# Low parts of split float32 weights: a subtraction on VectorE, or a negated copy on ScalarE and an adding DMA

## Chip, cores and metric

The kernel runs on one core of one Trainium2 chip. The metric is the device time of one execution in microseconds (us); the median of the runs counts.

## What is computed

One decoder layer for 512 tokens of width 1024, all in float32:

```python
h = x + 0.5 * swiglu(rmsnorm(h, ffn1_norm), w_gate, w_up, w_down)        # d_ff 2816
aq, ak, av, gq, gk, gv, glr, gog = split_cols(rmsnorm(h, mix_norm) @ w_in)
attn_o = sliding_window_attention(rope(aq), rope(ak), av, sinks)          # 8 heads of 64, window 128
gla_o  = rmsnorm(gla_chunked(gq, gk, gv, log_alpha), gla_out_norm) * silu(gog)
h = h + concat([attn_o, gla_o]) @ w_out
h = h + 0.5 * swiglu(rmsnorm(h, ffn2_norm), ...)                          # second feed-forward
h = h + sigmoid(rmsnorm(h, ple_gate_norm) @ ple_w_gate) * rmsnorm(p @ ple_w_proj, ple_norm)
```

## The kernel before

Every matmul of weights with activations is made of three on TensorE. Weight and activation are each held as a pair (`hi`, `lo`) of type float32r whose sum is the float32 value, and `mm3` adds hi x hi, hi x lo and lo x hi into one PSUM tile. So each weight must be loaded, cast to `hi`, and its rest computed as `lo`, before TensorE can use all of it.

The class `Weights` does that for all 88 units of up to 1 MB, in the order of their use. `load` starts a unit's DMA from DRAM on SP's queue into a raw tile `wraw`; there are two raw buffers, so the load of a unit waits until the unit two before it has been split. `split` makes one or two ring tiles of 128x1024 out of a unit (170 in all): ScalarE casts into `whi` (line 87), then VectorE writes `wlo` = raw - hi (line 88; GpSimd for units 2 and 3). Ring tiles lie in two rings, `whi` and `wlo`, of 5 buffers each. A new tile can only be written when TensorE has finished with the tile that had its buffer. `get` asks for splits up to 4 units ahead.

A unit is cut in one of two ways. `add_cols` units (gate and up weights, `in` columns of the mixer) hold 8 row blocks by 256 columns; a ring tile is 128 of these columns, so in the raw tile it is 8 separate pieces of 128 floats per partition. `add_rows` units (down projection, the other mixer weights, `w_out`, the last gate) give ring tiles of two whole row blocks of 512 columns, contiguous in the raw tile.

A feed-forward (`ffn`) runs over three groups of 8, 8 and 6 blocks of 128 hidden columns (`GROUPS`). For each pair of blocks TensorE goes through four ring tiles one after the other (gate, up, gate, up; PSUM tiles `pg`, `pu`), each with 24 matmuls of 512 columns. ScalarE and VectorE turn the results into the activation pairs `ahi`, `alo`. Then the down projection of the group: for each half of the output columns (c0 = 0, 512) four ring tiles (three in the last group) are used together by four GEMMs, one for each 128 tokens (PSUM tile `pd`). A GEMM takes the tiles in turn, six matmuls each, so the buffers of the four tiles come free one after the other while the fourth GEMM runs. The mixer and `w_out` use sets of four tiles in the same way (`gemm_ts`).

The order of instructions on each engine is set when the program is built, by a scheduler that places instructions by a timeline of its own; each engine then works through its list in order and waits on semaphores. GpSimd's list holds the powers of the row norms (`rs_...`, line 203) and some DMAs; SP's the loads.

Of the kernel before, what the change touches and what calls it, by code (L numbers as in the profile page):

```python
# [8 lines left out]
F32 = mybir.dt.float32  # L9
# [3 lines left out]
ALU = mybir.AluOpType  # L13
AX = mybir.AxisListType

P = 128
# [12 lines left out]
class Weights:  # L29
    """Streams weight units from DRAM and splits each into two float32r parts whose sum is the float32 weight."""  # L30

# [11 lines left out]
    def add_cols(self, name, w, c0, nf):  # L43
        """[1024, nf*128] columns: one ring tile [P, 8, 128] per 128 columns."""
        keys = [(name, c0 // P + i) for i in range(nf)]
        src = w[:, c0:c0 + nf * P].rearrange("(k p) c -> p k c", p=P)
        self.add(keys, [P, KC, nf * P], [(slice(0, P), src)], [
            (lambda r, i=i: r[:, :, i * P:(i + 1) * P]) for i in range(nf)])

    def add_rows(self, name, w, k0, nk, c0, n, tag=None):  # L50
        """nk row blocks of 128 by n columns: one ring tile [P, 2, n] per two row blocks."""
        src = w[k0 * P:(k0 + nk) * P, c0:c0 + n].rearrange("(k p) c -> p k c", p=P)
        keys = [(name, c0 if tag is None else tag, k0 + i) for i in range(0, nk, 2)]
        self.add(keys, [P, nk, n], [(slice(0, P), src)], [
            (lambda r, i=i: r[:, i:i + 2, :]) for i in range(0, nk, 2)])
# [16 lines left out]
    def split(self):  # L72
        nc = self.nc
        u = self.done
        while self.loaded <= u:
            self.load()
        keys, shape, loads, views = self.units[u]
        raw = self.raws[u]
        self.done += 1
        for i, (k, view) in enumerate(zip(keys, views)):  # L80
            v = view(raw)
            a, b = v.shape[1], v.shape[2]
            hi_t = self.ringp.tile([P, 1024], F32R, name=f"whi{u}_{i}", tag="whi")
            lo_t = self.ringp.tile([P, 1024], F32R, name=f"wlo{u}_{i}", tag="wlo")
            hi = hi_t[:, :a * b].rearrange("p (a b) -> p a b", a=a)
            lo = lo_t[:, :a * b].rearrange("p (a b) -> p a b", a=a)
            nc.scalar.copy(hi, v)  # L87
            (nc.gpsimd if u in (2, 3) else nc.vector).tensor_tensor(lo, v, hi.bitcast(F32), op=ALU.subtract)  # L88
            self.tiles[k] = (hi, lo)
# [8 lines left out]
def hymba_kernel(tc, A, out):  # L98
    nc = tc.nc
# [29 lines left out]
    def mm3(o, l, r, start, stop_):  # L129
        """o += l.T @ r where l and r are (hi, lo) pairs."""  # L130
        mm(o, l[0], r[0], start, False)
        mm(o, l[0], r[1], False, False)
        mm(o, l[1], r[0], False, stop_)

# [1 line left out]
    idn = cst.tile([P, P], F32, name="idn")  # L136
# [13 lines left out]

# [1 line left out]
    def add_ffn(i):  # L152
# [38 lines left out]

# [1 line left out]
    last_pow = [None]  # L193
# [6 lines left out]
    def rms_scale(ms, n, name):  # L200
        """(mean square + eps) ** -0.5"""
        rs = small(f"rs_{name}", n)
        last_pow[0] = nc.gpsimd.tensor_tensor(rs, ms, nhalf[:, :n], op=ALU.pow).ins
        return rs

    def norm(t, gain, nT, name):
        """Row norm of h[t], to be transposed into columns t*128.. of the (hi, lo) pair nT."""
        nrm = w4(f"nrm_{name}{t}")
        ss = small(f"ss_{name}{t}", 2)
        for c in range(2):  # L210
            sl = slice(c * 512, c * 512 + 512)
            nc.scalar.activation(nrm[:, sl], h[t][:, sl], AF.Square, scale=1.0 / 32.0, accum_out=ss[:, c:c + 1])
        ms = small(f"ms_{name}{t}", 1)
        nc.vector.scalar_tensor_tensor(ms, ss[:, 0:1], EPS, ss[:, 1:2], ALU.add, ALU.add)
        rs = rms_scale(ms, 1, f"{name}{t}")
        nc.vector.scalar_tensor_tensor(nrm, h[t], rs, gain, ALU.mult, ALU.mult)
        return t, nrm, nT, name
# [18 lines left out]
    def gemm_ts(ps, xT, t, tiles):  # L236
        """ps[tokens of t, n] = x[t] @ W, with x's transpose stationary; tiles hold two row blocks each."""
        n = len(tiles)
        for j, (wh, wl) in enumerate(tiles):
            for i in range(2):  # L240
                k = 2 * j + i
                mm3(ps, (xT[0][:, k, tokens(t)], xT[1][:, k, tokens(t)]), (wh[:, i, :], wl[:, i, :]),
                    k == 0, k == 2 * n - 1)
# [45 lines left out]

# [1 line left out]
    emb_d = [drp.tile([P, D], F32, name=f"emb_d{t}") for t in range(NT)]  # L291
# [45 lines left out]

# [1 line left out]
    consts = tc.issue_after(W.last_dma)  # L339
# [34 lines left out]

# [1 line left out]
    with tc.tile_pool(name="ffn1p", bufs=1, reuse_waits="tile") as fp:  # L376
# [13 lines left out]

# [1 line left out]
    hpool.close()  # L392
# [12 lines left out]
    def head_scale(src, name):  # L405
        """Per row and head of 64: (sum of squares + 64 eps) ** -0.5"""
        sq = t2(f"sq_{name}")
        nc.scalar.activation(sq, src, AF.Square)
        ss = small(f"qs_{name}", 8)
        nc.vector.reduce_sum(ss, heads(sq), AX.X)  # L410
        nc.vector.tensor_scalar_add(ss, ss, 64.0 * EPS)
        return rms_scale(ss, 8, f"q_{name}")

    def rotate(x, tab, wide, name):
        """Rotary embedding of x (views by wide) with the gains folded into the tables."""
        t1 = t2(f"r1_{name}")
# [7 lines left out]

    # keys, values and gate ranks of all tokens
    kall = t2("kall")
# [19 lines left out]

    # log decays of the recurrence and their running sums within chunks of 128 tokens
    glT = t2("glT")[0:17, :]
# [25 lines left out]

    # sliding-window attention; query heads are kept as pairs (h, h + 4), one per key head
    qTs = {}
# [71 lines left out]

    # gated linear attention
    gqT = mp.tile([P, 2, S], F32, name="gqT")  # L550
# [30 lines left out]

    # decayed scores of each chunk, transposed, by halving: pairs split at the middle of blocks of 2s tokens
    Ac = [mp.tile([P, 8, 64], F32, name=f"Ac{p}") for p in range(2)]
# [49 lines left out]

    # decayed queries, keys and the state after each chunk
    qb = mp.tile([P, 2, S], F32, name="qb")
# [132 lines left out]

# [1 line left out]
    hp = hpool.enter_context(tc.tile_pool(name="hp2", bufs=1, reuse_waits="tile"))  # L770
# [28 lines left out]

# [1 line left out]
    with tc.tile_pool(name="outp", bufs=1, reuse_waits="tile") as op:  # L801
# [30 lines left out]
def _constants():  # L832
    """Tables that depend on the shapes alone: rotary angles and masks."""
    f = np.float32
# [45 lines left out]
```

## Time and profile before

| | us |
|---|---|
| median of 3 runs (lowest, highest) | 1035.73 (1035.29, 1036.16) |
| profiled execution, first to last instruction | 1034.1 |
| TensorE busy | 1020.0 |
| VectorE busy | 457.8 |
| ScalarE busy | 352.9 |
| GpSimd busy | 45.9 |
| line 87, cast to `whi`, 170 on ScalarE | 176.5 |
| line 88, `wlo`, 166 on VectorE | 200.5 |

For the profiled execution the trace gives its span from first to last instruction; the median of the runs is 1.6 us more, which lies around the span. The busy times are sums over the span and overlap each other. Matmuls are pipelined: one is listed with 0.39 us although the next begins 0.23 us after it, so rates are read from distances between starts.

### The profile page before, as it was taken

What the parts mean: (1) busy time and instruction counts of PE and PEld (TensorE: products, weight loads), DVE (VectorE), ACT (ScalarE), POOL (GpSimd) and SP (SyncE); (2) the same over time, 40 slices, a digit from 0 to 9 for tenths busy, and PEclk for the clock granted to TensorE, in tenths of its full rate; (3) what the DMA queues carried; (4) which work ended last, traced back from release to release, by engine and by line L of the source; (5) the groups of instructions that cost most, each with busy time, mean ns of one, the idle gap of its engine ahead of it and who ended that gap; (6) DMA issues with size and microseconds to landing.
All of it is one profiled execution on the core that took longest, in us unless ns stands there. A gap on an engine that the chain in (4) does not pass through costs nothing.

```text
span 1034.1 us, 12380 instructions
## 1 busy us (share of the span) xinstructions
PE 1020.0 (99%) x5210; PEld 840.9 (81%) x5210; DVE 457.8 (44%) x610; ACT 352.9 (34%) x559; POOL 45.9 (4%) x58
## 2 busy tenths in 40 slices
PE   7999999999999999999999999999999999999998
PEld 5988888888888889887667779888888888888887
DVE  5533224333343346577876464332343323432553
ACT  6533113321132225554465243221132311332441
POOL 3300000000000001100000110000000000000100
PEclk9999999999999999999999999999999999999999
DMA  6842223322233234130203323332242222423231
GB/s 243 273 137 82 82 82 126 118 82 82 82 123 102 82 114 153 42 123 4 79 22 82 123 89 110 107 96 68 82 158 86 84 79 82 138 86 102 90 145 52
DMA packets 78203, 105.78 MB, mean 102 GB/s; under 512 B 5682, under 2 KB 55107, under 8 KB 78147
## 3 DMA queue, kind: packets, MB, share of 16 engines
q1 hardware_dynamic: 75842, 96.60, 28.6%
q0 software_dynamic: 2304, 8.39, 2.2%
q8 instruction: 41, 0.67, 0.3%
q14 instruction: 16, 0.12, 0.0%
HBM read 98.69 MB, written 6.29 MB: 102 GB/s over the span
## 4 chain that ended last, share of the span: by engine, by line
PE 97%; DVE 1%; ACT 1%; DMA 0%; issue 0%; SPq 0%
PE pg L127 23%; PE pu L127 23%; PE pd L127 23%; PE pgt L127 4%; PE wo L127 4%; PE gog L127 2%; PE gv L127 2%; PE gqk L127 2%; PE aq L127 2%; PE gr L127 1%; PE sc L127 1%; PE pv L127 1%; PE kvr L127 1%; PE o L127 1%; PE pe L127 1%; PE pt L540 1%
## 5 line engine op out<-in xcount | busy, mean ns | idle before, releaser
L87 ACT CAST whi<-wraw 128x1024 fp32r<-128x1024 f32 (+1 forms) x170 | 176.5, 1043 | 505.8 <-PE pg L127 144.7
L88 DVE TENSOR_TENSOR wlo<-wraw,whi 128x1024 fp32r<-128x1024 f32 (+1 forms) x166 | 200.5, 1212 | 215.1 <-ACT whi L87 205.4
L127 PE MATMUL pg<-nhi_f,whi 128*128 128x512 f32 (+1 forms) x384 | 143.3, 373 | 2.3 <-ACT nhi_f L196 2.3
L127 PE MATMUL pg<-nlo_f,whi 128*128 128x512 f32 (+1 forms) x384 | 143.6, 374 | 0.0
L127 PE MATMUL pu<-nhi_f,whi 128*128 128x512 f32 (+1 forms) x384 | 142.8, 372 | 0.5 <-DVE h L784 0.5
L127 PE MATMUL pg<-nhi_f,wlo 128*128 128x512 f32 (+1 forms) x384 | 143.1, 373 | 0.0
L127 PE MATMUL pu<-nlo_f,whi 128*128 128x512 f32 (+1 forms) x384 | 142.8, 372 | 0.0
L127 PE MATMUL pu<-nhi_f,wlo 128*128 128x512 f32 (+1 forms) x384 | 142.6, 371 | 0.0
L127 PE MATMUL pd<-whi,ahi 128*128 128x512 f32 x352 | 137.3, 390 | 0.2
L127 PE MATMUL pd<-wlo,ahi 128*128 128x512 f32 x352 | 137.0, 389 | 0.0
L127 PE MATMUL pd<-whi,alo 128*128 128x512 f32 x352 | 136.0, 389 | 0.0
L269 DVE TENSOR_TENSOR af<-pu,sg 128x512 f32<-128x512 f32 x44 | 30.4, 691 | 137.1 <-PE pu L127 136.7
L127 PEld LDWEIGHTS pg<-nhi_f,whi 128*128 128x128 f32 x384 | 72.7, 189 | 15.3 <-ACT nhi_f L196 3.0
L127 PEld LDWEIGHTS pu<-nhi_f,whi 128*128 128x128 f32 x384 | 72.5, 189 | 13.1 <-DVE h L784 0.7
L127 PEld LDWEIGHTS pg<-nhi_f,wlo 128*128 128x128 f32 x384 | 72.9, 190 | 12.6
L127 PEld LDWEIGHTS pg<-nlo_f,whi 128*128 128x128 f32 x384 | 72.8, 190 | 12.6 <-DVE nlo_f L197 0.2
L127 PEld LDWEIGHTS pu<-nlo_f,whi 128*128 128x128 f32 x384 | 72.5, 189 | 12.5
L127 PEld LDWEIGHTS pu<-nhi_f,wlo 128*128 128x128 f32 x384 | 72.3, 188 | 12.5
L286 DVE SCALAR_TENSOR_TENSOR h<-pd,h 128x512 f32<-128x512 f32 x48 | 33.1, 689 | 108.8 <-PE pd L127 108.8
L127 PEld LDWEIGHTS pd<-whi,ahi 128*128 128x128 f32 x352 | 66.1, 188 | 14.6 <-DVE h L286 1.1
L127 PEld LDWEIGHTS pd<-whi,alo 128*128 128x128 f32 x352 | 66.1, 188 | 13.8
L127 PEld LDWEIGHTS pd<-wlo,ahi 128*128 128x128 f32 x352 | 66.1, 188 | 13.6
(228 smaller groups left out, 1167.6 us busy)
## 6 DMA issues: line engine op xcount, KB each, us to landing
wraw<-in_ffn_w_gate_dram SPq DMA_DIRECT2D x22, 1024.0 KB, 5.1
wraw<-in_ffn_w_up_dram SPq DMA_DIRECT2D x22, 1024.0 KB, 5.2
wraw<-in_ffn_w_down_dram SPq DMA_DIRECT2D x20, 1024.0 KB, 5.0
wraw<-in_w_in_dram SPq DMA_DIRECT2D x8, 1024.0 KB, 5.2
wraw<-in_ple_w_gate_dram SPq DMA_DIRECT2D x4, 1024.0 KB, 5.3
h<-in_x_dram SPq DMA_DIRECT2D x4, 512.0 KB, 8.5
emb_d<-eo POOLq DMA_DIRECT2D x4, 512.0 KB, 4.6
wraw<-in_ffn_w_down_dram SPq DMA_DIRECT2D x4, 512.0 KB, 3.5
```

Of the source, the lines that this page charges most:

```text
L87: nc.scalar.copy(hi, v)
L88: (nc.gpsimd if u in (2, 3) else nc.vector).tensor_tensor(lo, v, hi.bitcast(F32), op=ALU.subtract)
L127: nc.tensor.matmul(o, lhsT=l, rhs=r, start=start, stop=stop_, **kw)
L269: nc.vector.tensor_mul(af, pu, sg)
L286: nc.vector.scalar_tensor_tensor(hs, ps, 0.5, hs, ALU.mult, ALU.add)
L540: nc.tensor.transpose(pt[:, tokens(a)], e[:, a, kb * P:(kb + 1) * P], idn)
```

## The change

Only `Weights.split` changes (and comments go, which moves later lines by 6). Units 0 and 1 and the last four (the whole last gate) keep the subtraction on VectorE, units 2 and 3 the one on GpSimd. For the other 80 units ScalarE writes the negated raw weights, rounded to float32r, into `wlo`; then a DMA on GpSimd's queue adds the raw weights to them in place, from SBUF to SBUF. So `wlo` again holds the weight less its rounding.

```diff
@@ Weights.split
             nc.scalar.copy(hi, v)
-            (nc.gpsimd if u in (2, 3) else nc.vector).tensor_tensor(lo, v, hi.bitcast(F32), op=ALU.subtract)
+            if u in (0, 1) or u > len(self.units) - 5:
+                nc.vector.tensor_tensor(lo, v, hi.bitcast(F32), op=ALU.subtract)
+            elif u in (2, 3):
+                nc.gpsimd.tensor_tensor(lo, v, hi.bitcast(F32), op=ALU.subtract)
+            else:
+                nc.scalar.mul(lo, v, -1.0)
+                nc.gpsimd.dma_start(out=lo.bitcast(F32), in_=v, accum_op=ALU.add)
```

The program then has 156 such copies on ScalarE (line 93) and 156 such DMAs on GpSimd (line 94): 88 of 128x8x128, 64 of 128x1024, 4 of 128x544. VectorE has 10 subtractions left. In the changed program SP's loads wait on the semaphores of these DMAs, where they waited on VectorE before.

ScalarE, first feed-forward, between the halves of the first group's down projection. The names are ring tiles (`whi`, `wlo`) and raw tiles (`wraw`) with their buffer numbers. Before:

```order
L272 CAST ahi_7_1049<-af_7_1047 128x512
L87 CAST whi_1_923<-wraw_917 128x1024
L87 CAST whi_0_929<-wraw_927 128x1024
L87 CAST whi_1_933<-wraw_927 128x1024
L87 CAST whi_0_1055<-wraw_1053 128x1024
```

In the changed program:

```order
L278 CAST ahi_7_1069<-af_7_1067 128x512
L93 ACTIVATE wlo_1_941<-wraw_933 128x1024
L87 CAST whi_1_940<-wraw_933 128x1024
L93 ACTIVATE wlo_0_948<-wraw_945 128x1024
L87 CAST whi_0_947<-wraw_945 128x1024
L93 ACTIVATE wlo_1_953<-wraw_945 128x1024
L87 CAST whi_1_952<-wraw_945 128x1024
L87 CAST whi_0_1075<-wraw_1073 128x1024
```

Each tile now has two instructions here, and the one for the low part stands ahead of the cast.

TensorE, at the start of the second half of the same down projection (`pd_0_512_0` is the GEMM of the first 128 tokens, `pd_0_512_1` of the next). Before, from the second tile's last matmuls on:

```order
L127 MATMUL pd_0_512_0_1197<-wlo_1_924,ahi_3_777 128x512
L127 MATMUL pd_0_512_0_1197<-whi_1_923,alo_3_778 128x512
L127 MATMUL pd_0_512_0_1197<-whi_0_929,ahi_4_905 128x512
L127 MATMUL pd_0_512_0_1197<-wlo_0_930,ahi_4_905 128x512
L127 MATMUL pd_0_512_0_1197<-whi_0_929,alo_4_906 128x512
L127 MATMUL pd_0_512_0_1197<-whi_0_929,ahi_5_913 128x512
L127 MATMUL pd_0_512_0_1197<-wlo_0_930,ahi_5_913 128x512
L127 MATMUL pd_0_512_0_1197<-whi_0_929,alo_5_914 128x512
```

In the changed program:

```order
L133 MATMUL pd_0_512_0_1225<-wlo_1_941,ahi_3_789 128x512
L133 MATMUL pd_0_512_0_1225<-whi_1_940,alo_3_790 128x512
L133 MATMUL pd_0_512_0_1225<-whi_0_947,ahi_4_921 128x512
L133 MATMUL pd_0_512_1_1251<-whi_0_935,ahi_0_641 128x512
L133 MATMUL pd_0_512_1_1251<-wlo_0_936,ahi_0_641 128x512
L133 MATMUL pd_0_512_1_1251<-whi_0_935,alo_0_642 128x512
...
L133 MATMUL pd_0_512_1_1251<-whi_1_940,alo_3_790 128x512
L133 MATMUL pd_0_512_1_1251<-whi_0_947,ahi_4_921 128x512
L133 MATMUL pd_0_512_0_1225<-wlo_0_948,ahi_4_921 128x512
```

After one matmul with the third tile's high part the next GEMM's first 12 matmuls, on the two tiles that are there, now go ahead of the third tile's low part.

TensorE, at the start of the second group's gate and up. Before, behind the 24 matmuls of the first gate tile:

```order
L127 MATMUL pg_8_1321<-nhi_f_96,wlo_0_1056 128x512
L127 MATMUL pu_8_1322<-nhi_f_96,whi_0_1065 128x512
L127 MATMUL pu_8_1322<-nlo_f_97,whi_0_1065 128x512
L127 MATMUL pu_8_1322<-nhi_f_96,wlo_0_1066 128x512
L127 MATMUL pu_8_1322<-nhi_f_96,whi_0_1065 128x512
L127 MATMUL pu_8_1322<-nlo_f_97,whi_0_1065 128x512
```

In the changed program:

```order
L133 MATMUL pg_8_1353<-nlo_f_97,whi_0_1075 128x512
L133 MATMUL pg_8_1353<-nhi_f_96,wlo_0_1076 128x512
L133 MATMUL pu_8_1354<-nhi_f_96,whi_0_1087 128x512
L133 MATMUL pu_8_1354<-nlo_f_97,whi_0_1087 128x512
L133 MATMUL pg_9_1355<-nhi_f_96,whi_1_1080 128x512
L133 MATMUL pg_9_1355<-nlo_f_97,whi_1_1080 128x512
...
L133 MATMUL pg_9_1355<-nlo_f_97,whi_1_1080 128x512
L133 MATMUL pg_9_1355<-nhi_f_96,wlo_1_1081 128x512
L133 MATMUL pg_9_1355<-nhi_f_96,whi_1_1080 128x512
```

Seven matmuls of the second gate tile (`pg_9`) have moved between the first two of the up tile (`pu_8`) and the first that needs its low part.

GpSimd, at the start of the second feed-forward: the reads of h, then the powers of its row norms (`rs_f`). Before:

```order
L773 DMA h_2_4427<-h_d_401 128x1024
L773 DMA h_3_4428<-h_d_402 128x1024
L203 TENSOR_TENSOR rs_f_4616<-ms_f_4614,nhalf 128x1
L203 TENSOR_TENSOR rs_f_4651<-ms_f_4649,nhalf 128x1
L203 TENSOR_TENSOR rs_f_4700<-ms_f_4698,nhalf 128x1
L143 DMA gain_ple_gate_norm<-in_ple_gate_norm_dram 128x1024
L203 TENSOR_TENSOR rs_f_4749<-ms_f_4747,nhalf 128x1
```

In the changed program:

```order
L94 DMA wlo_0_4533<-wraw_4530 128x8x128
L94 DMA wlo_1_4538<-wraw_4530 128x8x128
L209 TENSOR_TENSOR rs_f_4714<-ms_f_4712,nhalf 128x1
L209 TENSOR_TENSOR rs_f_4749<-ms_f_4747,nhalf 128x1
L209 TENSOR_TENSOR rs_f_4798<-ms_f_4796,nhalf 128x1
L94 DMA wlo_0_4545<-wraw_4542 128x8x128
L94 DMA wlo_1_4550<-wraw_4542 128x8x128
L94 DMA wlo_0_4661<-wraw_4658 128x8x128
L149 DMA gain_ple_gate_norm<-in_ple_gate_norm_dram 128x1024
L209 TENSOR_TENSOR rs_f_4847<-ms_f_4845,nhalf 128x1
```

Adding DMAs of 128x8x128 now stand ahead of the powers and, three of them, between the third and the fourth.

## Rows read from the trace of the kernel before

**Rows 1.** Page: busy us, share, instructions per engine; then the chain by engine.

```profile
PE 1020.0 (99%) x5210; PEld 840.9 (81%) x5210; DVE 457.8 (44%) x610; ACT 352.9 (34%) x559; POOL 45.9 (4%) x58
...
PE 97%; DVE 1%; ACT 1%; DMA 0%; issue 0%; SPq 0%
```

**Rows 2.** Windows by stage: stretch, us, busy us by engine, clock, DMA.

```profile
core 0: us, PE busy (x) PEld busy (x) DVE busy (x) ACT busy (x) POOL busy (x), PEclk, DMA share, GB/s
0.00:20.00 20.00, 14.58 (x56) 11.85 (x57) 11.27 (x16) 10.74 (x24) 2.40 (x10) 1.00 0.87 315
20.00:45.00 25.00, 22.83 (x170) 21.99 (x169) 11.66 (x17) 15.86 (x32) 14.89 (x11) 0.93 0.60 194
45.00:380.00 335.00, 334.90 (x1504) 278.19 (x1504) 120.00 (x137) 91.06 (x113) 1.20 (x3) 1.00 0.32 103
...
560.00:640.00 80.00, 78.17 (x441) 66.33 (x441) 41.66 (x65) 27.89 (x52) 9.35 (x13) 1.00 0.31 103
640.00:990.00 350.00, 349.89 (x1570) 290.21 (x1569) 131.15 (x146) 99.34 (x129) 4.32 (x8) 1.00 0.32 105
990.00:1034.00 44.00, 39.63 (x203) 33.48 (x201) 17.17 (x25) 9.67 (x15) 0.00 (x0) 1.00 0.13 51
```

**Rows 3.** Timeline of PE: start us, us, line, operation, out<-in, shapes.

```profile
111.64 0.39 PE L127 MATMUL pu<-nhi_f,whi 128*128 128x512 f32 x1
...
117.08 0.39 PE L127 MATMUL pd<-whi,ahi 128*128 128x512 f32 x1
...
138.84 0.39 PE L127 MATMUL pd<-whi,ahi 128*128 128x512 f32 x1
...
140.43 0.39 PE L127 MATMUL pd<-wlo,ahi 128*128 128x512 f32 x1
```

**Rows 4.** Groups: count | busy us, mean ns | idle us before.

```profile
L87 ACT CAST whi<-wraw 128x1024 fp32r<-128x1024 f32 (+1 forms) x170 | 176.5, 1043 | 505.8 <-PE pg L127 144.7
L88 DVE TENSOR_TENSOR wlo<-wraw,whi 128x1024 fp32r<-128x1024 f32 (+1 forms) x166 | 200.5, 1212 | 215.1 <-ACT whi L87 205.4
...
L601 ACT ACTIVATE X<-X 128x1024 f32<-128x1024 f32 x7 | 7.4, 1061 | 2.1 <-DVE X L600 2.1
```

**Rows 5.** GpSimd: its DMAs on emb_d with landing; two timeline rows.

```profile
L336 POOL DMA_DIRECT2D emb_d<-eo x4: 533/533/611, 42.2 to 45.8; - x4
...
DMA to landing us min/median/max: 3.5/4.6/6.6
...
578.78 2.17 POOL L773 DMA_DIRECT2D h<-h_d  x4
...
619.64 0.56 POOL L203 TENSOR_TENSOR rs_f<-ms_f,nhalf 128x1 f32<-128x1 f32 x1 [1.56 <-DVE ms_f L214]
```

**Rows 6.** DMA, 145 to 187 us: packets, MB, share; issues with landing.

```profile
q1 hardware_dynamic: 4160, 4.19, 30.5%
...
wraw<-in_ffn_w_gate_dram SPq DMA_DIRECT2D x2, 1024.0 KB, 5.1
```

**Rows 7.** DMA, 92 to 135 us: loads for the down projection.

```profile
q1 hardware_dynamic: 1584, 3.15, 21.9%
```

**Rows 8.** DMA, 578 to 590 us: the queue of GpSimd.

```profile
q0 software_dynamic: 576, 2.10, 49.8%
```

**Rows 9.** Timeline of ScalarE around the first down projection.

```profile
111.61 1.05 ACT L87 CAST whi<-wraw 128x1024 fp32r<-128x1024 f32 x1 [3.79 <-PE pg L127]
...
135.02 1.05 ACT L87 CAST whi<-wraw 128x1024 fp32r<-128x1024 f32 x1 [16.32 <-PE pd L127]
136.37 1.05 ACT L87 CAST whi<-wraw 128x1024 fp32r<-128x1024 f32 x1 [0.30 <-PE pd L127]
```

**Rows 10.** Timeline of VectorE, subtractions at the same place.

```profile
136.10 3.95 DVE L88 TENSOR_TENSOR wlo<-wraw,whi 128x1024 fp32r<-128x1024 f32 x3 [1.80 <-ACT whi L87]
```

**Rows 11.** Windows of 5 us near the start, columns as in group 2.

```profile
20.00:25.00 5.00, 3.17 (x19) 2.53 (x17) 1.68 (x4) 5.00 (x8) 4.64 (x3) 1.00 0.00 0
25.00:30.00 5.00, 4.66 (x27) 4.46 (x28) 1.78 (x3) 4.94 (x13) 4.99 (x4) 0.67 0.39 106
```

## The prediction

> **What bounds the kernel now.** I read the page's busy shares first, then the chain that ended last, then the stretches by stage, then single instructions around two places where the weight ring turns over. TensorE is busy 1020.0 of 1034.1 us and the chain is 97% TensorE [rows 1]. From 45 to 380 and from 640 to 990 us it idles 0.1 us in each stretch, and from 560 to 640 us 1.8 us [rows 2]. So the middle of the kernel has about 2 us to win at most; the other 12 us of idle time lie in the first 45 and the last 44 us [rows 2], whose weight units keep the old code. VectorE with 457.8 us and ScalarE with 352.9 us [rows 1] wait for TensorE, so taking work from VectorE shortens nothing by itself. The question is only whether the new way of making `wlo` stays hidden.
>
> What hides it now is the ring. One tile of gate or up weights is 24 matmuls; the first of one stands at 111.64 and of the next at 117.08 us, so a tile lasts 5.44 us and a matmul 0.227 us [rows 3]. The low part costs VectorE 1.21 us, the cast before it 1.04 us on ScalarE [rows 4]. In gate and up a slot comes free four tiles (21.8 us) before its next content is used. It is tight only where four tiles are used together by four GEMMs, as in the down projection: there slots come free 1.36 us apart (six matmuls), during the last GEMM.
>
> **What is removed and added.** 156 subtractions leave VectorE: 156 x 1.21 = 189 us of an engine that waits, worth 0 on the path. ScalarE gets 156 scaled copies. The nearest row is an ACTIVATE of 128x1024 with 1.06 us [rows 4], so 165 us, to some 518 us of the span: half, and beside matmuls. GpSimd gets 156 DMAs, 88 of them (gate, up and `in` columns) in pieces of 512 bytes, 1024 per DMA (a load with rows of 1 KB makes 4160 / 4 = 1040 packets of its 1 MB [rows 6], so pieces follow the rows), and 68 in whole rows, 128 per DMA (4 of these are 544 wide). The raw tile is now held until that DMA has landed, not until the subtraction ends, so SP's load of the unit after next waits for it as well.
>
> *Issue.* A DMA of 128 rows holds GpSimd 0.53 us, and four in a row take 2.17 us [rows 5]. No row shows 1024 pieces. Bounds: 0.53 (pieces cost nothing) and 8 x 0.53 = 4.26 us (all of it is pieces). An operation on 128x1 takes the same engine 0.55 us [rows 5], which speaks for a large fixed part; that four DMAs take four times one shows no start-up that could overlap. I take the upper end, since a piece must be listed one by one and nothing in the rows shows it for nothing. If the accumulation needs its destination listed as a second source, twice 4.26 = 8.5 us is the far end.
>
> The Trainium skill (DMA: Bandwidth & Descriptors, Anatomy of one DMA) says that a lot of descriptors can be emitted before their cost shows. By it the issue would be near 0.53 us and the sum near that of the second rival below. No run here shows it.
>
> *Transfer.* A load in pieces of 1 KB had its engines busy 30.5% of 42 us: 0.305 x 42 x 16 / 4160 = 49 ns a piece; in pieces of 2 KB 0.219 x 43 x 16 / 1584 = 95 ns; GpSimd's own rows of 4 KB 0.498 x 12 x 16 / 576 = 166 ns [rows 6 to 8]. So time goes with bytes, about 46 ns for 1 KB. An accumulation may read both source and destination: a piece of 512 bytes then costs between 25 ns (half the 1 KB piece) and 2 x 49 = 99 ns, and a tile of 64 pieces per engine 1.6 to 6.3 us. I take two reads by bytes, 49 ns and 3.2 us; for a tile in whole rows 1.3 to 2.7 us. Gate and up then need 3.2 + 1.6 (half a unit's load) = 4.8 us of the engines for each 5.44 us.
>
> The Trainium skill (Collectives: The Full Stack, The bandwidth ceiling) says that an add in a DMA halves the rate since it reads two sources; by it the tile is 3.2 us, without it 1.6, and the DMA term of the raw loop below falls by a half. No trace here shows an accumulation.
>
> *Landing.* GpSimd's DMAs of the same 512 KB land 3.5 us (least) or 4.6 us (median) after issue [rows 5], against DRAM; I use 4.6, and 4.1 after the end of a long issue.
>
> **Where it reaches the path,** with the order of the changed program as the front shows it:
>
> A. Second half of the down projection, 6 times. The first freed slot starts work on ScalarE at 135.02; the low part is needed by the matmul at 140.43 [rows 3, 9]. Before, VectorE had it by 137.4 (136.10 + a third of 3.95) [rows 10]. Now the copy ends at 136.08 and lands at 139.6 with 3.5, 140.7 with 4.6, 142.0 with the second read's 1.3 on top: a wait of 0 to 1.6 us. Later tiles are covered by the rearranged matmuls (12 of the next GEMM go ahead). 6 x 1.0 = 6 us.
>
> B. Down projection to the next gate and up, 4 times, and the start of the second feed-forward: 5. From the start of the last GEMM slots come free at 1.36, 2.72 and 4.08 us; the copies end at 2.4, 4.5 and 6.7 (copy and cast take turns); issues of 4.26 run to 6.7, 10.9, 15.2; the first up tile lands at 15.0. TensorE wants it after 5.44 (GEMM) + 5.44 (gate tile) + 9 moved matmuls (2.0) = 12.9. Wait 2.1, with 3.5 us landing 1.0. 5 x 2.1 = 10.5 us.
>
> C. Gate and up to the down projection, 6 times. The last of the four tiles is cast at 111.61 [rows 9]; copied by 113.7, landed by 119.7; needed 18 matmuls and one after 117.08, at 121.4. Covered by 1.7 us, unless one strided issue of 4.26 stands before it on GpSimd, or its load is late. 0 to 4.2, taken 2: 12 us.
>
> D. In the mixer seven sets of four tiles follow each other (`kvr`, `aq`, `in`, `gv`, `gog`, `wo` twice), each like A: 7 x 1.0 = 7 us (0 to 14).
>
> E. The raw loop of gate and up. A raw buffer goes round once in four tiles, 21.8 us: load, copy 2.1, two issues 8.5, landing 4.1. The load is 5.1 us alone [rows 6], plus 0.4 to issue; beside one accumulation on the same engines 3.2 more. 5.5 + 2.1 + 8.5 + 4.1 = 20.2 fits, 23.4 misses by 1.6. 88 / 4 = 22 rounds: 0 to 36 us; I take 36, since the engines are 88% taken by the count above.
>
> F. At the start of the second feed-forward the powers of `rs_f` stand on GpSimd between strided DMAs and wait for their issues; before, each took 0.56 us there [rows 5]. One issue late: 4 us (0 to 8.5).
>
> G. The clock. After the idle 1.8 us between 20 and 25 us the granted clock was 0.67 in the next 5 us [rows 11], a third of the way up from the lower level (1.2 GHz) to full 2.4 GHz, 1.65 us of work lost; the 1.8 us idle between 560 and 640 show no drop [rows 2]. Each long wait may cost 0 to 1.65 more; taken 0, kept in the range (20 waits: 33 us).
>
> Sum: 6 + 10.5 + 12 + 7 + 4 + 36 = 75.5 us. The profile's span is 1034.1, and the median of the runs 1035.7, 1.6 us of it outside the span and untouched. Forecast 1035.7 + 75.5 = 1111 us, and 1050 to 1175 for this case (its upper ends: 9.6 + 10.5 + 25 + 14 + 36 + 8.5 + 33 = 137).
>
> **Rivals.** *GpSimd's issue becomes the bound.* At 8.5 us an issue, four tiles need 34 us against 21.8: 22 x 12.3 = 270, and with A, C, D and F some 40 more: 1345 us. It decides from 5 us on (the raw loop) and in full from 5.44 us, each further 0.1 us costing 8.8 us. For it: the destination has to be read as well. Against: no row. Between 5 and 8.5 us lies 1175 to 1345.
>
> *Everything stays hidden.* With an issue near 0.53, one read's time and a landing of 3.5 us, A, B, C and E vanish; 0 to 14 us remain of D and F: 1036 to 1050. For it: every margin above is positive at the best bounds. Against: all must hold at once, and half of F alone is as much as a measurement can see. The sentence of the Trainium skill above would end here.
>
> *The DMA engines become the bound.* If each 512-byte read costs a whole 1 KB piece, 6.3 + 1.6 = 7.9 us for each 5.44: 88 x 2.5 = 217, with turns 257: 1293 us. It decides from 3.8 us a tile. Against: the three piece sizes show time by bytes.
>
> *Faster.* VectorE's relief could only take the 1.8 us around 600 us: 1034 us, if VectorE's queue causes them and nothing else comes late.
>
> **How the numbers follow.** About 0.2% (2 us) is what a measurement can tell from no change. Forecast's case 0.51; issue bound 0.25; hidden 0.12 (5 in 100 of it within 2 us, the rest slower by 2 to 14); engines bound 0.10; faster 0.02. So faster 0.02, same 0.05, slower 0.93. The range leaves out a tenth below 1045 (hidden, faster) and a tenth above 1300 (the upper part of the issue-bound case): 1045 to 1300.
>
> **What would show it.** In the changed profile: GpSimd's DMA of 128x8x128 against that of 128x1024 gives the issue (4.26 against 0.53 right, 8.5 or 0.6 wrong); packets and share of the software queue give the transfer (49 ns a piece); TensorE's waits should name `wlo`, in gate and up more than in the down projection; SP's loads should wait for GpSimd's DMAs. An idle TensorE in every gate and up tile, not at turns, means that one of the two bounds holds. If TensorE stays busy but its clock is lower, G was sized wrong. A time under 1045 us would make the issue of small pieces the wrong step.

## The result and the profile after

| us | before | changed |
|---|---|---|
| median of the runs | 1035.95 | 1132.68 |
| least and most | 1035.29, 1040.31 | 1121.46, 1135.98 |
| profiled execution, span | 1034.1 | 1129.9 |

The ratio over the runs is 1.0902, 95% interval 1.0859 to 1.0944: slower by 9%. The median lies 21.7 us above the forecast of 1111 us and inside the range of 1045 to 1300. The page of the changed kernel, busy time per engine, GpSimd's DMA queue (packets, MB, share), and the chain that ended last; the first and the last answer to [rows 1]:

```profile
PE 1056.8 (94%) x5210; PEld 861.2 (76%) x5210; DVE 278.2 (25%) x454; ACT 485.3 (43%) x713; POOL 240.1 (21%) x214
...
q0 software_dynamic: 103616, 89.21, 51.3%
...
DMA 43%; issue 24%; PE 21%; ACT 6%; POOL 4%; DVE 1%; SPq 0%; POOLq 0%; ACTq 0%; DVEq 0%
```

The span grew by 95.8 us, and TensorE's row splits that in two. Its idle time went from 1034.1 - 1020.0 = 14.1 to 1129.9 - 1056.8 = 73.1 us, so 59.0 us are new waits. Its busy time, for the same 5210 matmuls, grew by 1056.8 - 1020.0 = 36.8 us: they ran at a lower clock (the mean granted clock is 0.961, before 0.998). The waits of TensorE, by what ended them (us in total, times, longest):

```profile
PE pd L133 <- DMA wlo<-wraw: 16.9, 5, 5.6
PE pg L133 <- ACT whi L87: 12.1, 4, 3.1
PE ntr_f L229 <- DVE nlo_f L203: 8.0, 2, 6.8
PE pd L133 <- ACT ahi L278: 6.6, 2, 3.4
...
PE gqk L133 <- DMA wlo<-wraw: 2.5, 1, 2.5
```

Most of these stand at turns: the six places where gate and up hand over to the down projection (`pd`), four where the down projection hands over to the next gate (`pg`), and the start of the second feed-forward (`ntr_f`). Inside gate and up TensorE hardly waits: from 310 to 380 us it is busy all the time with the adding DMAs running. Windows of the changed kernel (columns as in [rows 2]), two at a turn and that one:

```profile
125.00:130.00 5.00, 2.61 (x6) 2.13 (x7) 0.69 (x1) 2.51 (x3) 0.85 (x1) 0.66 0.52 102
130.00:135.00 5.00, 5.00 (x16) 3.94 (x16) 0.69 (x1) 0.00 (x0) 0.00 (x0) 0.66 1.03 261
...
310.00:380.00 70.00, 70.00 (x310) 57.63 (x309) 7.62 (x11) 31.43 (x37) 18.69 (x13) 1.00 0.97 174
```

The second window has no idle time at all, and 16 matmuls where 5 us at full clock hold 22: the granted clock was 0.66 behind the wait in the first. The 36.8 us arise in such stretches; e7 below tests whether the waits cause them.

Why the turns are late is seen on SP. Its loads for the first down projection in the changed kernel (start, us; each waits until its raw buffer is free):

```profile
98.90 0.37 SPq L69 DMA_DIRECT2D wraw<-in_ffn_w_down_dram  x1
108.04 0.37 SPq L69 DMA_DIRECT2D wraw<-in_ffn_w_down_dram  x1
118.13 0.37 SPq L69 DMA_DIRECT2D wraw<-in_ffn_w_down_dram  x1
127.48 0.37 SPq L69 DMA_DIRECT2D wraw<-in_ffn_w_down_dram  x1
```

and the first and the last of the same four in the kernel before:

```profile
81.36 0.37 SPq L69 DMA_DIRECT2D wraw<-in_ffn_w_down_dram  x1
...
113.95 0.37 SPq L69 DMA_DIRECT2D wraw<-in_ffn_w_down_dram  x1
```

They are issued 17.5 to 13.5 us later. The load at 108.04 takes the buffer of a unit whose last adding DMA was issued at 96.48: 11.6 us went on landing, beside the load of 98.90. ScalarE then waits for the loads in order, with everything else it has to do behind them, as its timeline shows (answers to [rows 9]):

```profile
108.20 1.05 ACT L87 CAST whi<-wraw 128x1024 fp32r<-128x1024 f32 x1 [11.59 <-DMA wraw<-in_ffn_w_down_dram]
...
125.11 1.04 ACT L87 CAST whi<-wraw 128x1024 fp32r<-128x1024 f32 x1 [7.03 <-DMA wraw<-in_ffn_w_down_dram]
126.06 1.05 ACT L93 ACTIVATE wlo<-wraw 128x1024 fp32r<-128x1024 f32 x1
127.02 0.60 ACT L278 CAST ahi<-af 128x512 fp32r<-128x512 f32 x1
...
158.79 1.04 ACT L87 CAST whi<-wraw 128x1024 fp32r<-128x1024 f32 x1 [9.32 <-DMA wraw<-in_ffn_w_gate_dram]
```

The row at 127.02 has nothing to do with weights: the last activations of gate and up were ready, and stood behind a cast that waited for a load.

The wait at this first turn (the 5 us windows above) ended on the low part of the fourth down tile. ScalarE cast that tile at 115.60, 4.0 us later than before, and its adding DMA landed 9.5 us after its issue, beside the load of 118.13 (timelines of GpSimd and TensorE):

```profile
117.89 0.85 POOL L94 DMA_DIRECT2D wlo<-wraw  x1 [1.57 <-ACT wlo L93]
...
127.39 0.80 PE L133 MATMUL pd<-wlo,ahi 128*128 128x512 f32 x1 [3.25 <-DMA wlo<-wraw]
...
128.84 0.63 PE L133 MATMUL pd<-wlo,ahi 128*128 128x512 f32 x1
129.27 0.63 PE L133 MATMUL pd<-whi,alo 128*128 128x512 f32 x1
```

So this wait has two parts, a late load and a slow landing.

The row at 158.79 is the first gate tile of the second group, and TensorE meets it in the middle of the down projection (its timeline):

```profile
156.42 0.39 PE L133 MATMUL pd<-whi,ahi 128*128 128x512 f32 x1
159.88 0.50 PE L133 MATMUL pg<-nhi_f,whi 128*128 128x512 f32 x1 [3.08 <-ACT whi L87]
160.22 0.39 PE L133 MATMUL pg<-nlo_f,whi 128*128 128x512 f32 x1
160.45 0.40 PE L133 MATMUL pd<-wlo,ahi 128*128 128x512 f32 x1
...
175.02 0.39 PE L133 MATMUL pd<-whi,alo 128*128 128x512 f32 x1
175.25 0.39 PE L133 MATMUL pg<-nhi_f,wlo 128*128 128x512 f32 x1
```

Two gate matmuls stand ahead of 58 down matmuls, 13 us of work that was ready while TensorE waited 3.08 us. In the kernel before the first gate matmul stands behind the last of `pd`. This is an effect of the change on the order that the prediction had not looked at.

### The profile page after: what moved, and what is told of

Same layout as the page of the kernel before. It is cut to its first block, busy times and chain, and to the rows that moved or that the text cites. A ratio compares the mean times of both kernels' runs of the same rounds, so it can differ in the third digit from the quotient of the medians.

```text
span 1129.9 us, 12747 instructions
## 1 busy us (share of the span) xinstructions
PE 1056.8 (94%) x5210; PEld 861.2 (76%) x5210; DVE 278.2 (25%) x454; ACT 485.3 (43%) x713; POOL 240.1 (21%) x214
## 4 chain that ended last, share of the span: by engine, by line
DMA 43%; issue 24%; PE 21%; ACT 6%; POOL 4%; DVE 1%; SPq 0%; POOLq 0%; ACTq 0%; DVEq 0%
DMA wlo<-wraw 17%; DMA wraw<-in_ffn_w_gate_dram 15%; DMA wraw<-in_ffn_w_down_dram 7%; PE pd L133 4%; PE pgt L133 4%; PE wo L133 3%; POOL wlo L94 3%; ACT wlo L93 3%; PE pu L133 2%; PE pg L133 2%; ACT whi L87 2%; DMA wraw<-in_w_out_dram 2%; DMA wraw<-in_w_in_dram 2%; PE aq L133 1%; PE o L133 1%
## 5 line engine op out<-in xcount | busy, mean ns | idle before, releaser
L94 POOL DMA_DIRECT2D wlo<-wraw x156 | 194.9, 1249 | 725.1 <-ACT wlo L93 677.4
L93 ACT ACTIVATE wlo<-wraw 128x1024 fp32r<-128x1024 f32 (+1 forms) x156 | 162.9, 1044 | 138.8 <-PE pd L133 117.9
L133 PE MATMUL pd<-wlo,ahi 128*128 128x512 f32 x352 | 146.7, 417 | 16.9 <-DMA wlo<-wraw 16.9
L133 PE MATMUL pg<-nhi_f,whi 128*128 128x512 f32 (+1 forms) x384 | 145.1, 378 | 16.2 <-ACT whi L87 12.1
L133 PE MATMUL pd<-whi,ahi 128*128 128x512 f32 x352 | 143.3, 410 | 7.3 <-ACT ahi L278 6.6
L133 PE MATMUL pd<-whi,alo 128*128 128x512 f32 x352 | 143.5, 411 | 0.0
L279 DVE TENSOR_TENSOR alo<-af,ahi 128x512 fp32r<-128x512 f32 x44 | 30.4, 692 | 282.6 <-ACT ahi L278 282.5
L133 PEld LDWEIGHTS pd<-wlo,ahi 128*128 128x128 f32 x352 | 71.1, 202 | 35.5 <-DMA wlo<-wraw 20.5
L133 PEld LDWEIGHTS pd<-whi,ahi 128*128 128x128 f32 x352 | 70.4, 200 | 25.1 <-ACT ahi L278 7.5
L133 PEld LDWEIGHTS pd<-whi,alo 128*128 128x128 f32 x352 | 70.8, 201 | 15.2
L133 PEld LDWEIGHTS pu<-nlo_f,whi 128*128 128x128 f32 x384 | 72.5, 189 | 12.6
```

The lines of the kernel that those rows point to most:

```text
L93: nc.scalar.mul(lo, v, -1.0)
L94: nc.gpsimd.dma_start(out=lo.bitcast(F32), in_=v, accum_op=ALU.add)
L133: nc.tensor.matmul(o, lhsT=l, rhs=r, start=start, stop=stop_, **kw)
L279: nc.vector.tensor_sub(alo, af, ahi.bitcast(F32))
```

## Experiments

The theories. **Held buffer**: a raw buffer is free only when the adding DMA that reads it has landed, so loads start late. **Crowded engines**: the adding DMAs slow the loads down. **Late low part**: copy, issue and landing of `wlo` take longer than the subtraction. **ScalarE's pass**: the copies delay the rest of its queue. The runs stand in the order in which their readings are needed.

| run | median, us | ratio to before, 95% interval |
|---|---|---|
| e8_room | 1035.80 | 0.9993 (0.9978 to 1.0008) |
| e9_load_only | 1040.09 | 1.0023 (1.0002 to 1.0045) |
| e2_act_only | 1044.16 | 1.0080 (1.0063 to 1.0097) |
| e4_cols_only | 1051.97 | 1.0150 (1.0128 to 1.0171) |
| e10_raw3_order | 1066.09 | 1.0274 (1.0239 to 1.0309) |
| e6_turns | 1070.86 | 1.0321 (1.0283 to 1.0358) |
| e3_rows_only | 1074.86 | 1.0383 (1.0331 to 1.0434) |
| e11_neg_dve | 1094.18 | 1.0539 (1.0497 to 1.0581) |
| e12_raw2_order | 1111.73 | 1.0696 (1.0638 to 1.0754) |
| e7_fill | 1111.75 | 1.0732 (1.0684 to 1.0780) |
| e1_raw3 | 1117.10 | 1.0783 (1.0767 to 1.0799) |
| e5_hold_only | 1152.38 | 1.1090 (1.1047 to 1.1134) |

### Holding against loading: e5 and e9

```diff
# e5_hold_only, on the kernel before, behind the subtraction; sc is one of two scratch tiles in turn (their making is left out)
+                nc.gpsimd.tensor_copy(sc[:, 0:1, 0:1], hi.bitcast(F32)[:, 0:1, 0:1])
+                nc.gpsimd.dma_start(out=sc, in_=v, accum_op=ALU.add)
# e9_load_only: the same on gate, up and down units, src a slice of nT1 or mixT in the same pieces
+                nc.gpsimd.dma_start(out=sc, in_=src, accum_op=ALU.add)
```

> The kernel before, its low parts by VectorE as before, with an adding DMA of each raw tile into one of two scratch tiles that nobody reads (behind a one-element copy on GpSimd from whi, so that it starts where the changed kernel's does). It has the held raw buffer and the load on the DMA engines, and neither ScalarE's second pass nor a later low part. Held buffer: the four waits of 3 us at down projection -> gate and up come back, for ScalarE's cast behind a late load, little at gate and up -> down projection (there the column-only and the row-only kernel each had none): 1046 to 1065 us. Late low part or ScalarE's pass as the cause: 1037 to 1043. Crowded DMA engines: as held buffer, but with waits in the middle of gate and up too.

> The hold kernel with another source: the adding DMAs into the scratch tiles read 512-byte pieces or whole rows of the normalised activations, which nobody overwrites meanwhile, and not the raw buffer (128 of the 156, those of gate, up and down; the mixer and ple_gate have none). The engines carry the same traffic at the same places and no raw buffer is held. Held buffer: nearly all of the hold kernel's loss goes, 1037 to 1052 us. Crowded DMA engines: the loads are as late as there, 1100 to 1150, in the two feed-forwards.

e5 took 1152.38 us and e9 1040.09 us; e5 missed its expectation upwards, e9 met it. The two differ in what the DMA reads (and e9 has none in the mixer). What ScalarE waits for in e5, then in e9, and the first down load of each on SP:

```profile
ACT whi L88 <- DMA wraw<-in_ffn_w_gate_dram: 197.9, 20, 13.0
ACT whi L88 <- DMA wraw<-in_ffn_w_down_dram: 147.7, 18, 11.3
ACT whi L88 <- DMA wraw<-in_ffn_w_up_dram: 102.1, 16, 13.6
...
103.23 0.37 SPq L70 DMA_DIRECT2D wraw<-in_ffn_w_down_dram  x1
```

```profile
ACT whi L88 <- DMA wraw<-in_ffn_w_gate_dram: 47.3, 11, 6.1
ACT whi L88 <- DMA wraw<-in_ffn_w_up_dram: 20.0, 4, 5.9
...
83.14 0.37 SPq L70 DMA_DIRECT2D wraw<-in_ffn_w_down_dram  x1
```

With the same traffic in the feed-forwards, but no raw buffer held, the loads keep their time (83.14 against 81.36 before) and TensorE is late by 1.8 us at the end of the first feed-forward; with the buffers held it is late by 40.3 (table below). The loads do land later beside the adding DMAs, before and in e9 (median, us):

```profile
wraw<-in_ffn_w_down_dram SPq DMA_DIRECT2D x20, 1024.0 KB, 5.0
...
wraw<-in_ffn_w_down_dram SPq DMA_DIRECT2D x20, 1024.0 KB, 7.6
```

Started in time, they cost little even so. That excludes crowded engines as the cause by themselves; slower landings can still lengthen the hold. e5 also makes its low parts on VectorE, at once, and still loses more than the changed kernel: a late low part isn't needed for the loss. Its waits are for `ahi` (31.8 us) and `whi`, as a queue behind late loads makes them. It is no measure of the changed kernel's hold, though: its two scratch tiles let GpSimd wait 148.6 us for their DMAs, so it holds longer.

### One buffer more, and the order: e1, e12, e10

```diff
# e1_raw3, on the changed kernel (e10 has it too)
-    rawp = pool("rawp", 2)
+    rawp = pool("rawp", 3)
# e12_raw2_order, on the changed kernel; e10_raw3_order, on e1: last_mm is the last matmul written
+                    with tc.issue_after(last_mm[0]) if f0 and fa == f0 else ExitStack():
                         for j in range(2):
```

> The changed kernel with three raw buffers instead of two (room made by one t2 buffer less in the mixer and one sg and one af buffer less in the second feed-forward, so the first feed-forward, to about 560 us, is the clean part). Four theories for TensorE's new waits of about 3 us at the turns. Held buffer: a raw buffer is not free until the adding DMA has read it and landed, so the next load is issued 9 to 12 us later than before, and ScalarE waits for it; then a third buffer takes away the four waits of 3 us at down projection -> gate and up (12 us), those of the 24 us at gate and up -> down projection that end on a late raw load, and the clock's fall behind them: 1070 to 1095 us. Late low part: the way copy, issue, landing to wlo is longer than VectorE's subtraction: turns stay as they are, 1125 to 1135. Crowded DMA engines: the load itself is slow beside the adding DMAs: 1125 to 1140, waits the same or longer. ScalarE's second pass: 1125 to 1135.

> The three-raw-buffer kernel with the first gate and up matmuls behind a down projection tied behind its last matmul: in the three-buffer kernel 20 matmuls of the next gate stand in the written order of TensorE ahead of the last down matmul (2 in the changed kernel), so that the waits of 4 to 5 us on wlo come while 18 us of other work is left. Held buffer and an order that took its gain: the four waits of 4 to 5 us go, with their clock 1085 to 1100 us; the short ones in the second and fourth tile behind (1 to 3 us) may stay. Crowded DMA engines alone: the waits only move behind the down projection, 1112 to 1120.

> The changed kernel with its two raw buffers and the same tie as in the three-buffer kernel with order (the first gate and up matmuls behind the last down matmul): what the tie does by itself. Held buffer: the loads are as late as before, so the waits of 3 us at down projection -> gate and up stay (only 2 matmuls change places), and so do those at gate and up -> down projection: 1122 to 1138 us, and the step from here to the three-buffer kernel with order (1066) is the buffer's. If the order alone did it: 1066 to 1090.

e1 missed: 1117.10 us. All its waits at gate and up -> down projection are gone but two of 0.6 us for `h`, as a held buffer wants; but at down projection -> gate and up TensorE waits more, as here:

```profile
159.37 0.80 PE L133 MATMUL pg<-nhi_f,wlo 128*128 128x512 f32 x1 [5.31 <-DMA wlo<-wraw]
```

with down matmuls behind it from 165.15 on: 20 gate matmuls had moved ahead of the last down matmul, where the changed kernel has two. e10 ties them behind it and takes 1066.09 us, below its expectation of 1085 to 1100: the waits of up to 5 us go, and also the short ones behind them.

e12 missed as well, and taught most: 1111.73 us, where I expected the tie of two matmuls to do nothing. The four waits of 3 us are gone, though the loads are as late as they were (98.62 for the first down load). So they were made by two things together, the late load and the two moved matmuls, and either one undone takes them away: in e9 two gate matmuls stand early too, but the gate load starts at 139.12 us (149.57 in the changed kernel) and TensorE does not wait for it.

The order moved in other runs too. By TensorE's timelines, the gate matmuls ahead of the last down matmul of the first group are none before and in e4, e5 and e6, two in the changed kernel, e9 and e11, 13 in e2, and 20 in e1 and e3. So e1 and e3 hold a price of the order as well, and only the runs with the tie separate it.

The waits at gate and up -> down projection stay in e12 and go in e10. Where the time lies, from the start of the first matmul of `kvr`, of `wo` and of `pgt` in each trace:

| us | before | changed | e12 | e10 | e5 | e9 |
|---|---|---|---|---|---|---|
| first feed-forward, to `kvr` | 390.4 | 423.9 | 413.7 | 394.1 | 430.7 | 392.2 |
| mixer, `kvr` to `wo` | 171.4 | 184.7 | 184.7 | 184.0 | 191.4 | 171.4 |
| `wo` and second feed-forward | 420.8 | 467.8 | 461.2 | 434.9 | 477.9 | 422.4 |
| `pgt` to the end of the span | 51.5 | 53.5 | 53.5 | 53.5 | 51.6 | 51.6 |

In medians the order is 1132.7 - 1111.7 = 21.0 us and the third buffer with the order tied 1111.7 - 1066.1 = 45.6 us. The 32 us by which e10's span is still longer than before's lie in the mixer (12.6), in `wo` and the second feed-forward (14.1) and elsewhere (5.7). In the mixer the new waits that can be named are those for a low part: 1.6 and 1.1 us (`aq`), 2.5 (`gqk`), 2.9 (`gog`). So the longer way to `wlo` does count there. e8_room shows that the room taken for the third buffer (and for the scratch tiles of e5 and e9) costs nothing:

> The kernel before with the buffers that the three-raw-buffer and the hold kernels gave up (t2 five instead of six, in the second feed-forward one sg and one af instead of two): the price of that room. All theories: 1036 to 1040 us; what is above 1036 is to be taken off those two kernels' times.

It took 1035.80 us.

### Small edits at the turns: e6

```diff
-            if u in (0, 1) or u > len(self.units) - 5:
+            if u in (0, 1) or u > len(self.units) - 5 or keys[0] in TURN:
```

> The changed kernel with VectorE's subtraction back for 24 of its units alone: the last gate and the last up unit ahead of each down projection and the units of each down projection's second half, those whose raw buffers the first loads of the next stage need. Held buffer: TensorE's waits at both kinds of turn (24 and 12 us of them in the changed kernel) fall to 5 us in all or less, and the clock's fall behind them goes: what is left is the mixer, the start of the second feed-forward and the clock there, 1052 to 1075 us. Late low part: gate and up -> down projection keeps its waits (first down units still by DMA): 1085 to 1105. Crowded DMA engines: in proportion to the DMAs left (110 of 156): 1095 to 1110.

It took 1070.86 us, as the held buffer wants, and no wait over 0.6 us is left at the two kinds of turn (one of 8.3 us remains at the start of the second feed-forward). It keeps the adding DMAs on the first down units. The two gate matmuls don't move in it either, so it undoes the order as well and doesn't separate the two.

### Columns, rows, ScalarE: e4, e3, e2, e11

```diff
# e4_cols_only (e3_rows_only has == KC)
+            if u in (0, 1) or u > len(self.units) - 5 or (u > 3 and shape[1] != KC):
# e2_act_only, on the changed kernel
                 nc.scalar.mul(lo, v, -1.0)
-                nc.gpsimd.dma_start(out=lo.bitcast(F32), in_=v, accum_op=ALU.add)
+                nc.vector.tensor_tensor(lo, v, hi.bitcast(F32), op=ALU.subtract)
# e11_neg_dve, on the changed kernel
-                nc.scalar.mul(lo, v, -1.0)
+                nc.vector.tensor_scalar_mul(lo, v, -1.0)
```

> The change for the column units alone (gate, up, in: 1024 pieces of 512 bytes a tile); the units of whole rows are subtracted on VectorE as before. Held buffer: the waits at down projection -> gate and up go (raw buffers of down units come free after one cast), those at gate and up -> down projection stay where the down units' loads wait for the last gate and up tiles' adding DMAs: 6 waits of 2 to 4 us and the clock behind them, 1055 to 1080 us. Late low part: only in, 1038 to 1045, since gate and up tiles are needed long after they land. Crowded DMA engines: nearly the whole loss, 1100 to 1130. The raw loop of gate and up (term E of the prediction, 36 us): 1070 with short waits in every round.

> The change for the units of whole rows alone (down projection, kvr, aq, gv, gog, wo: one piece of 4 KB per partition and tile); the column units (gate, up, in) are subtracted on VectorE as before. Held buffer: the gate unit behind a down projection is still late, so the waits of 3 us at down projection -> gate and up stay (12 us), and gate and up -> down projection waits only for the landing of its first wlo (0 to 2 us each, 0 to 12), mixer about 9: with the clock 1065 to 1095 us. Late low part: nearly all of the loss stays, 1100 to 1130. Crowded DMA engines (the bulk of the pieces is in gate and up): 1040 to 1055.

> The kernel before with ScalarE's negated pass added for each of the 156 tiles; VectorE then subtracts as before and overwrites its result, no adding DMA. This is the price of ScalarE's second pass (2.1 us per tile for cast and pass together) in its queue ahead of ahi and sg, without any DMA. ScalarE's second pass as the cause: half or more of the loss, 1080 us or more, with waits of TensorE for ahi. Held buffer, late low part, crowded engines: 1036 to 1045 us.

> The changed kernel with the negated pass on VectorE and not on ScalarE, the adding DMA as it is. Held buffer: ScalarE's casts still wait in order for late loads with ahi and nhi_f behind them, so the turns stay: 1115 to 1135 us. ScalarE's second pass as the cause: the waits for ahi and the start of the second feed-forward go, 1060 to 1100. Late low part: the copy starts up to 1 us earlier, 1115 to 1130.

e4 took 1051.97 us, below its range: no turn waits, not even those I had left to it (its order has no early gate matmuls). Its largest new wait is one of 4.8 us at 56 us. So the 512-byte pieces in the steady part of gate and up are hidden. e3 took 1074.86 us, with four waits at down projection -> gate and up (1.5 to 3.1 us) and none at the other turn. The two halves of the change, e3 and e4, lose 39.0 and 16.1 us, together 55 of 96.7: neither has the six waits at gate and up -> down projection, which so need both late loads, which the column units make, and a late low part or copy of the down units, which the row units add. This fits the two parts of the wait at 127.39.

ScalarE's pass costs 8 us by itself (e2, as expected) and far more with the DMA: e11 took 1094.18 us, 38.5 less than the changed kernel. It missed the 1115 or more that a held buffer alone would leave, and lies in the range of 1060 to 1100 set for ScalarE's pass as the cause. That theory is met in half: the waits for `ahi` are gone, but the one at the start of the second feed-forward grew from 6.8 to 11.3 us. Without the copies in ScalarE's queue the first feed-forward ends at 399.4 us (423.9), and the loads come earlier: the first gate load of the second group starts at 146.15 us (149.57), and TensorE does not wait for it, with the same two early matmuls. So the pass and the held buffer work together. In the changed kernel ScalarE's copies wait for ring slots that the down projection still uses, ahead of its other work:

```profile
ACT wlo L93 <- PE pd L133: 117.9, 11, 16.0
```

That this is the way by which they cost 38 us is argued from the row, not shown: in e11 the cast and the negated pass also no longer take turns on one engine.

### The clock: e7

```diff
+    def fill(ps, nT):
+        with tc.issue_after(last_mm[0]):
+            for k in range(12):
+                mm(ps, nT[0][:, 0, 0:P], nT[0][:, k % KC, :], True, True)
```

> The changed kernel with 12 matmuls more of 128x512 (2.7 us) on TensorE at each of ten turns (six gate and up -> down projection, four down projection -> gate and up), results overwritten, behind the last matmul of the stage before: TensorE works in the time in which it waited. Clock lost because TensorE waits: the waits at the turns fall by 2 to 3 us each, the filler pays for itself, and the granted clock stays at 1.00 behind them: the 25 or so us of clock lost at the turns come back, 1100 to 1115 us. Clock lowered for another reason (the DMA traffic): 1130 to 1140, the clock at the turns still 0.5 to 0.7. Turns later by what the filler adds: 1145 to 1160.

It took 1111.75 us, as clock lost to waits would have it, though not for that reason alone: the filler also kept the two gate matmuls behind the down projection, as the tie of e12 does, so e12 is what to compare it with. Against e12 it has 10 x 2.72 = 27.2 us of filler, of which 16 stand where e12 waits, and the same time. Its windows at the first turn, then e12's at the same place:

```profile
125.00:130.00 5.00, 5.00 (x24) 4.14 (x23) 0.19 (x1) 0.00 (x0) 0.00 (x0) 1.00 0.98 251
130.00:135.00 5.00, 3.07 (x12) 1.62 (x11) 0.69 (x1) 2.51 (x3) 0.85 (x1) 1.00 0.39 64
135.00:140.00 5.00, 5.00 (x23) 4.11 (x23) 0.69 (x1) 0.00 (x0) 0.00 (x0) 1.00 0.97 257
```

```profile
125.00:130.00 5.00, 0.49 (x3) 0.07 (x1) 1.35 (x2) 4.17 (x5) 1.41 (x2) 1.00 1.08 307
130.00:135.00 5.00, 4.44 (x13) 3.49 (x14) 0.69 (x1) 0.66 (x2) 0.85 (x1) 0.66 1.05 208
```

A wait of 5 us is followed by a clock of 0.66; 2.7 us of useless matmuls in its place keep it at 1.00, even with the 1.9 us of waiting left at 133 us, and with the DMA engines busy 0.98 before that wait and 0.97 behind it. All six turns from gate and up to the down projection agree: in the 5 us behind each, the granted clock of e7 is 1.00 at a DMA share of 0.68 to 0.98; in e12 it is 0.50 to 0.69 behind five of the six. So at the turns the clock falls because TensorE waits.

## Why the prediction was right and where it was wrong

The sign, the range and the forecast's case held. The nearness of 1111 to 1132.7 us does not speak for the steps: two large errors, E and G, nearly cancel, which is luck. By terms, in the profiled execution:

| term | predicted | measured |
|---|---|---|
| A, second half of the down projection | 6 | 0 |
| B, down projection to gate and up | 8.4 of the 10.5 | 12.1 |
| C, gate and up to down projection | 12 | 24.2 |
| D, mixer | 7 | 11.6 |
| E, raw loop of gate and up | 36 | 2.2 |
| F, start of the second feed-forward, with B's fifth | 4 + 2.1 | 7.2 |
| G, clock | 0 | 36.8 |
| `ntr_pg`, not foreseen | 0 | 1.7 |

The measured waits add up to 59.0 us, and with G to the 95.8 us of the span.

*Issue.* This is the step that failed first. I took 4.26 us for 1024 pieces, since each must be listed, from the 0.53 us of 128 rows [rows 5]. GpSimd's row for the adding DMA (ns, least, median, most), with the landing behind it:

```profile
L94 POOL DMA_DIRECT2D wlo<-wraw x156: 847/1537/1637, 38.0 to 1057.8; - x156
...
wlo<-wraw POOLq DMA_DIRECT2D x152, 512.0 KB, 6.3
```

1.54 us for 1024 pieces and 0.85 for whole rows: 0.69 us for 896 pieces more, where my choice took 7 x 0.53 = 3.7. An adding DMA has a price of its own (0.85 against 0.53 for as many rows) and little per piece; that lay between my bounds, and I had not weighed it. The rule of the Trainium skill (DMA: Bandwidth & Descriptors, Anatomy of one DMA) that many descriptors can be emitted before their cost shows was nearer than my choice. The trace stands between the two. The rival of GpSimd as the bound falls with this.

*Transfer.* Right. While adding DMAs alone ran, from 218 to about 222 us, the engines moved 177 to 184 GB/s (40 slices of 218 to 226 us; the load issued at 221.02 joins them behind):

```profile
GB/s 184 182 184 184 182 184 182 184 182 177 177 179 184 184 182 184 182 184 179 184 184 182 184 177 172 182 184 172 161 154 156 146 172 202 215 236 246 246 246 246
```

183 GB/s over 16 engines is 512 bytes in 45 ns (49 predicted) and 2.9 us a tile (3.2). Loads took 49 ns for twice the bytes [rows 6]. The Trainium skill (Collectives: The Full Stack, The bandwidth ceiling) has the add of a reduction halve the rate, since it reads two sources; the trace agrees (45 ns for half the bytes). The landing was sized too small: 4.4 us least, 6.1 median and 11.5 most after the issue, where I used 4.6. The rival of the DMA engines as the bound falls with that and with e9.

*E and C.* The mechanism that E named, a raw buffer held until the DMA lands, is the one that counts (e5, e9, e10), but in another place. With issues of 1.54 us the round of four tiles fits: SP's gate loads follow each other by 19.9 and 21.8 us (57.18, 77.10, then a down load at 98.90), TensorE's own pace, so gate and up don't wait. But the loads have lost the lead that they had before, and it is missed at the turns, where the ring gives less time. My sign for E, waits for `wlo` in gate and up more than in the down projection, came out the other way round: 0.6 against 16.9 us. C had said "or its load is late" and priced that at 0 to 4.2 us: the value taken, 2, should have been the upper end, 4.0 each. It also counted 6.0 us from the end of the copy to the landing; at the first turn it was 9.8 (117.60 to 127.39).

*B.* The size was near, the mechanism wrong: no up tile waited behind long issues. A gate tile's load was late and two gate matmuls had been put 13 us too early. I had read the order behind the first gate tile (nine moved matmuls), not ahead of it.

*D.* The size was near for other reasons: 4.1 of the 11.6 us are waits for a low part (`aq` 1.6, `gqk` 2.5), the rest for ScalarE and VectorE, such as `o` with 3.4 and `gx` with 1.7.

*A and F.* A's waits didn't come: the moved matmuls covered them, as the order said they might. F's 6.8 us came, but not on GpSimd: the powers of `rs_f` ran in time (0.55 to 0.60 us each), and ScalarE's casts of `nhi_f` stood behind a copy that waited for a late gate load.

*G* was left at 0 although rows 11 showed 1.65 us lost behind an idle time of 1.8 us. 20 waits at up to 1.65 us, the 33 us that I kept in the range, came near the 36.8 in sum, though single waits differ: the clock took nothing behind one and about 2.8 us behind another (last section).

What stays open: how the last 30 us (medians of e10 and before) divide between late low parts, ScalarE and the clock, how ScalarE's pass makes a held buffer cost 38 us more (e11), and why the halves e3 and e4 fall 42 us short of the whole beyond what C explains.

## What to carry to other kernels

When an operation that reads a staging buffer moves to a DMA, count the buffer as held until the landing, and look at the places where several loads in a row need buffers, not at the steady loop: here the steady loop waited 2 us and the turns 36, before the clock behind them. Compare the written order ahead of each turn as well as behind it: two matmuls put early cost 21 us once their load came late. When a scheduler orders the program, look whether a test run has moved the order along with what it tests. A wait of 3 us on TensorE must be priced with the clock behind it, and a forecast that leaves that at nothing because it isn't certain will come out low.

## What the runs showed of the hardware

An adding DMA in SBUF from GpSimd holds the engine 0.85 us for 128 rows of 4 KB and 1.54 us for 1024 pieces of 512 bytes, moves 183 GB/s when it is alone, and lands 4.4 us (least) to 11.5 us (beside a load of 1 MB) after its issue. The clock does not answer each wait alike: in e3 two waits of 2.90 us of the same kind, at 147.6 and 281.7 us, were followed by these windows:

```profile
150.00:155.00 5.00, 4.45 (x19) 3.68 (x20) 2.61 (x3) 0.50 (x1) 0.00 (x0) 1.00 0.35 118
...
285.00:290.00 5.00, 5.00 (x17) 3.91 (x16) 2.21 (x3) 0.00 (x0) 0.00 (x0) 0.66 0.12 42
```

1.00 behind the first and 0.66 behind the second. At the lower of the two levels (1.2 of 2.4 GHz) the matmuls of 128x512 start 0.43 us apart instead of 0.23. So the clock behind a wait of about 3 us cost nothing in the first of these, and about 2.8 us behind the wait at 127.39 of the changed kernel, where 13 matmuls took the 5.7 us to 133.11.
